# Scores of a two-component attention: two passes over stacked high and low parts per component, or three passes per component on half of the array's rows

## The chip, the cores and the metric

The kernel runs on one core of a Trainium2 chip. The metric is device time in microseconds for one execution of the whole step. The core has a matrix engine (PE; its weight loads are shown apart, as PEld), a vector engine (DVE), an activation engine (ACT), a general engine (POOL) and a queue for transfers (SP). Each engine takes its instructions in a fixed order, and engines wait for one another through semaphores.

## The reference

One layer of a streaming encoder is computed for 16 meta tokens, 2048 new frames and, apart, 32 frames of a running stream. The change touches the attention of the 2048 frames, above all the first line below:

```python
s = jnp.einsum('bqhcd,bkhcd->bchqk', q, k, preferred_element_type=f32) * SCALE
bias = rel_bias[rel_bucket(k_pos[None, :] - q_pos[:, None])]
s = s + bias; s = where(chunk_id(k_pos) <= chunk_id(q_pos), s, NEG)
p = jax.nn.softmax(s, axis=-1)
a = p[:, 0] - lam * p[:, 1]
return jnp.einsum('bhqk,bkhd->bqhd', a.astype(v.dtype), v)
```

There are 4 heads. A head's query and key have 128 numbers, which are two components c of 64 numbers each. Each component gives its own scores and softmax, and the second softmax, times lambda, is taken from the first. Around this stand an RMS norm, one input projection to 4096 columns, a gated short convolution, an output projection, a residual and a final norm. All is float32.

## The kernel before, in words

**Numbers in two parts.** A float32 operand of a product is split into a high part (a cast to the matmul type float32r) and a low part (what the cast left out). A product of a and b is then the sum of high·high, high·low and low·high. In the projections each of these is one matmul (line 212), three per 128 rows of contraction.

**Stages.** The 2048 frames are worked in four stages p of 512 frames, and in each stage the four heads h follow one another. `unit_a(h, p)` projects keys, values, queries and gates of one head for 512 frames. `attend(h, p, st)` then takes the four query tiles t of 128 frames, in two steps of two tiles. `unit_c` does the convolution of a column tile behind it.

**Scores.** For a query tile the visible key columns (16 meta and t + 1 tiles of 128) are cut into chunks of 144 to 512 columns; over the run there are 176 chunks. For each chunk and each component c `softmax_diff` calls `mm` (lines 427 to 429), which writes 128 queries x w keys to a PSUM bank of the pool `ps_s` (3 banks). DVE takes the row minimum (line 378, or 375 with the bias), ACT the exponential (line 379), which frees the bank. Later POOL and DVE (lines 382 and 383) join the two components, PE transposes the result (line 444), ACT and DVE split it (447 and 448), and lines 451 to 453 multiply it with the values.

**How a component's 64 rows fill 128.** The key tile `ks[c]` holds in its rows 0 to 63 the high part of component c and in its rows 64 to 127 the low part. The query tiles `q{c}0` and `q{c}1` hold the high part of component c in both halves, and the low part in both halves. So line 428 gives high·high + high·low in one pass over all 128 rows, and line 429 gives low·high + low·low: two full passes for each component and four for each chunk, 704 matmuls in all. To bring the parts into these rows, the loop behind `proj(CQ + h, ...)` issues 8 transfers `q<-r` of 64 rows per unit, and the loop behind `proj(CK + h, ...)` copies 64 rows at a time into `ks`, from the new keys (`ks<-r`) and, for p > 0, from the older ones in DRAM (`ks<-ksd`).

**What sets the order.** The program text gives dependencies. A list scheduler, which simulates the engines while it builds the program, chooses the order in which each engine's instructions stand. It works on single instructions: it may put other work between two matmuls which the text has next to each other. On the chip the order of each engine is fixed. All transfers are issued on SP by one helper, line 73.

Of the kernel before, what the change touches and what calls it, by code (L numbers as in the profile page):

```python
# [11 lines left out]
F32 = mybir.dt.float32  # L12
# [5 lines left out]
P = 128  # L18
# [29 lines left out]
def hybrid_step(ctx: ExitStack, tc: tile.TileContext, x, xT, ckT, cv, scT, rel_bias, norm_g, w_in,  # L48
# [9 lines left out]
    gp = pool("gp", 8)  # L58
    rp = pool("rp", 5)
    op = pool("op", 3)  # L60
# [16 lines left out]

# [1 line left out]
    ident = const.tile([P, P], F32, name="ident")  # L79
# [16 lines left out]

# [82 lines left out]

# [1 line left out]
    pre = {}  # L181
# [33 lines left out]

# [1 line left out]
    ksd = [dram.tile([2, P, NK], F32, name=f"ksd{h}", tag=f"ksd{h}") for h in range(H)]  # L217
# [6 lines left out]
    def unit_a(h, p):  # L224
# [13 lines left out]
        dma(kT_p[h, :, k0:k0 + kn], k32[:, :kn])  # L238
        ks = [kv.tile([P, NK], F32R, tag=f"ks{c}", name=f"ks{c}") for c in range(2)]
        for c in range(2):  # L240
            for i, src in enumerate((kh, kl)):
                if p > 0:
                    dma(ks[c][64 * i:64 * i + 64, :k0], ksd[h][i, 64 * c:64 * c + 64, :k0])
                dma(ks[c][64 * i:64 * i + 64, k0:k0 + kn], src[64 * c:64 * c + 64, :kn])
        if p < NQ - 1:
# [58 lines left out]

        qh, ql, q32 = r_tile(tw), r_tile(tw), g_tile(tw)
        qs = None
# [11 lines left out]
        proj(CQ + h, p, ev_q)  # L318
        qd = []
        for c in range(2):  # L320
            pair = []
            for i, src in enumerate((qh, ql)):
                q2 = one.tile([P, QT], F32R, tag=f"q{c}{i}", name=f"q{c}{i}")
                for half in range(2):
                    dma(q2[64 * half:64 * half + 64], src[64 * c:64 * c + 64, f0:f0 + QT])
                pair.append(q2)
            qd.append(pair)
        st["q"] = qd
        st["qs"] = qs
# [9 lines left out]

# [22 lines left out]
    def softmax_diff(pn, chunks, mm, bz):  # L362
        """chunks: [(first column, width)]; mm(c, ps, col, w) writes negated scores, bz is the negated bias of the
        last 512 columns; returns the chunks of a."""
        nch = len(chunks)
# [3 lines left out]
        for j, (c0, w) in enumerate(chunks):  # L369
            pr.append([pp.tile([P, 512], F32, tag=f"p{c}", name=f"p{c}", bufs=NP[c])[:pn, :w] for c in range(2)])  # L370
            for c in range(2):
                s = ps_s.tile([P, 512], F32, tag="s", name="s")[:pn, :w]
                mm(c, s, c0, w)
                if j == nch - 1:
# [11 lines left out]
    def chunks_of(t):  # L386
        """The columns (16 meta, then t + 1 tiles of 128) in pieces of at most 512, cut between tiles."""
        n = t + 1
# [26 lines left out]
    def attend(h, p, st):  # L415
        (q0h, q0l), (q1h, q1l) = st["q"]
        qd = st["q"]
        ks, (vh, vl), (z32, l1) = st["ks"], st["v"], st["z"]
        f0 = NM if p == 0 else 0
        o32, sq = o_tile(), o_tile()  # L420
        for b in range(2):
            tl = [4 * p + 2 * b, 4 * p + 2 * b + 1]
            aa = []
            for t in tl:
                qs = slice(P * (t - 4 * p), P * (t - 4 * p + 1))

                def mm(c, ps, col, w):
                    T.matmul(ps, lhsT=qd[c][0][:, qs], rhs=ks[c][:, col:col + w], start=True, stop=False)  # L428
                    T.matmul(ps, lhsT=qd[c][1][:, qs], rhs=ks[c][:, col:col + w], start=False, stop=True)  # L429
                ch = chunks_of(t)  # L430
                aa.append((ch, softmax_diff(P, ch, mm, st["bz"])))
# [34 lines left out]
    def attend_sample(h, st):  # L466
        """Rows 0..31: component 0 of the queries; rows 32..63: component 1."""
        kts, cvt, q2, (z32, l1) = st["kts"], st["cvt"], st["qs"], st["z"]
# [38 lines left out]

# [1 line left out]
    def unit_c(u, p):  # L509
# [54 lines left out]

# [1 line left out]
    bvs, bzd = [], []  # L566
# [22 lines left out]
    def prep_small():  # L589
# [32 lines left out]

# [1 line left out]
    y0 = [dram.tile([P, 512], F32, name=f"y0_{t}", tag=f"y0_{t}") for t in range(17)]  # L624
    ssq0 = const.tile([P, 17], F32, name="ssq0")

    def w_half(n):
# [3 lines left out]
        else:  # L631
            ks = [kv.tile([P, NK], F32R, tag=f"ks{c}", name=f"wo{c}") for c in range(2)]
            his = [ks[k // 4][:, 512 * (k % 4):512 * (k % 4 + 1)] for k in range(KT)]
            los = [r_tile(512) for _ in range(4)]
            los += [one.tile([P, QT], F32R, tag=f"q{c}{i}", name=f"wq{c}{i}") for c in range(2) for i in range(2)]
        for k in range(KT):
# [24 lines left out]
    def half_product(y, c, w, rows, ssq):  # L661
        """y (the residual) += cat @ w for 512 columns, and the sum of its squares."""
        chh, cll = c
# [52 lines left out]

# [1 line left out]
    after = (((0,), (1,), (2, 3), ()), ((0,), (1,), (2,), (3,)))  # L718
# [74 lines left out]
```

## Time and profile before

| what | before |
|---|---|
| median of 3 timed runs | 1342.75 us (1339.35 to 1343.84) |
| profiled execution, span from the first to the last instruction | 1338.5 us |
| PE busy | 1285.5 us, 96% of the span |
| PEld busy | 1104.2 us, 82% |
| DVE, ACT, POOL busy | 999.3, 717.6, 682.8 us |
| score matmuls, lines 428 and 429 | 352 and 352 |
| transfers `q<-r` | 128, 128 KB each, 4.7 us to landing (median) |

The page gives the profiled execution's span and no second time for it; the 4.25 us between the span and the median of the timed runs are what lies around it, and the spread of the runs. In the profile L428 is a line of the kernel before. A row names the written tile, an arrow and the tiles read, then the stationary operand's rows*columns (128*64 is 128 rows and 64 columns) and the moving operand's rows x columns. The duration of a matmul holds its way through the array and overlaps with the next one. What one costs in a stream is the distance between two starts, which is called the pitch below.

### The profile page before, as it was taken

Reading aid. Unit: us, or ns where it says so; the run is one execution under the profiler, and the core shown is the slowest. Engines: PE = TensorE matmul, PEld = TensorE weight load, DVE = VectorE, ACT = ScalarE, POOL = GpSimd, SP = SyncE. Lnnn points to the kernel's source line nnn. Section 1 sums busy time; section 2 is a strip of 40 time slices with the busy share of each in tenths; the row PEclk is TensorE's granted clock in tenths of the full one; section 3 lists DMA queues with packets and bytes.
Section 4 is the critical chain, followed back from the end, with each engine's and each line's share of the span. In section 5 each row is a group of like instructions: output and inputs, shape, how many; then the busy total and the mean of one; then the engine's idle time right before and its main releaser. Section 6 shows DMA issues by size and latency. Waiting matters only on the chain.

```text
span 1338.5 us, 21190 instructions
## 1 busy us (share of the span) xinstructions
PE 1285.5 (96%) x7058; PEld 1104.2 (82%) x7058; DVE 999.3 (75%) x2086; ACT 717.6 (54%) x1814; POOL 682.8 (51%) x619
## 2 busy tenths in 40 slices
PE   8899999999999999999999999998999999999997
PEld 6899999977878878878878788887887877878875
DVE  8677676668887958788888898786785895777753
ACT  5554454555564547454645566465554665674432
POOL 4555556455555663565566535564574573452200
PEclk9999999999999999999999999999999999999999
DMA  8754543894445377545453463636247348445851
GB/s 276 229 155 125 164 117 104 245 274 138 139 147 158 103 209 232 141 151 150 150 135 126 120 208 93 167 124 143 94 110 203 117 160 215 165 150 185 273 196 52
DMA packets 118670, 215.59 MB, mean 161 GB/s; under 512 B 19840, under 2 KB 48032, under 8 KB 118560
## 3 DMA queue, kind: packets, MB, share of 16 engines
q1 hardware_dynamic: 118560, 214.23, 54.7%
q8 instruction: 56, 0.92, 0.3%
q14 instruction: 54, 0.44, 0.1%
HBM read 145.62 MB, written 43.26 MB: 141 GB/s over the span
## 4 chain that ended last, share of the span: by engine, by line
PE 59%; DVE 16%; DMA 10%; issue 4%; ACT 4%; POOL 3%; SPq 2%; DVEq 0%; POOLq 0%; ACTq 0%
PE pj L212 37%; PE po L676 6%; DVE p L383 3%; PE s L428 3%; DMA q<-r 3%; PE s L429 3%; PE pt L444 3%; SPq L73 2%; DVE nm L378 2%; PE po L452 2%; PE po L453 2%; PE po L451 2%; DMA ks<-ksd 1%; ACT p L379 1%; POOL wl L192 1%
## 5 line engine op out<-in xcount | busy, mean ns | idle before, releaser
L212 PE MATMUL pj<-xh,wh 128*128 128x512 f32 (+2 forms) x1280 | 457.0, 358 | 4.0 <-ACT wh L191 1.3
L192 POOL TENSOR_TENSOR wl<-wr,wh 128x512 fp32r<-128x512 f32 x240 | 328.7, 1375 | 250.2 <-ACT wh L191 234.7
L212 PE MATMUL pj<-xl,wh 128*128 128x512 f32 (+2 forms) x1280 | 455.1, 356 | 0.8 <-DVE xl L140 0.8
L212 PE MATMUL pj<-xh,wl 128*128 128x512 f32 (+2 forms) x1280 | 454.7, 356 | 0.0
L379 ACT ACTIVATE p<-s,nm 128x384 f32<-128x384 f32 (+5 forms) x352 | 208.8, 595 | 186.8 <-DVE nm L378 135.1
L212 PEld LDWEIGHTS pj<-xh,wh 128*128 128x128 f32 x1280 | 243.2, 190 | 34.2 <-ACT bvec L586 2.0
L212 PEld LDWEIGHTS pj<-xh,wl 128*128 128x128 f32 x1280 | 242.9, 190 | 31.2 <-issue 1.3
L212 PEld LDWEIGHTS pj<-xl,wh 128*128 128x128 f32 x1280 | 243.4, 190 | 30.1 <-DVE xl L140 1.4
L191 ACT CAST wh<-wr 128x512 fp32r<-128x512 f32 x256 | 157.0, 616 | 129.4 <-PE pj L212 78.6
L383 DVE SCALAR_TENSOR_TENSOR p<-p,cf,p 128x384 f32<-128x384 f32 (+5 forms) x176 | 174.5, 1019 | 28.1 <-POOL p L382 27.8
L428 PE MATMUL s<-ks,q 128*128 128x384 f32 (+5 forms) x352 | 129.5, 375 | 26.8 <-DMA q<-r 10.0
L382 POOL TENSOR_SCALAR p<-p,cf 128x384 f32<-128x384 f32 (+5 forms) x176 | 125.0, 726 | 49.2 <-DVE cf L359 35.1
L378 DVE TENSOR_REDUCE nm<-s 128x1 f32<-128x400 f32 (+3 forms) x224 | 122.5, 557 | 28.2 <-PE s L429 27.9
L429 PE MATMUL s<-ks,q 128*128 128x384 f32 (+5 forms) x352 | 124.0, 354 | 2.0 <-DMA q<-r 2.0
L448 DVE TENSOR_TENSOR al<-pt,ah 128x512 fp32r<-128x512 f32 x144 | 97.0, 682 | 37.0 <-ACT ah L447 36.9
L656 POOL TENSOR_TENSOR cll<-ct,chh 128x512 fp32r<-128x512 f32 x40 | 53.9, 1353 | 113.6 <-ACT chh L654 105.4
L428 PEld LDWEIGHTS s<-ks,q 128*128 128x128 f32 x352 | 66.2, 190 | 42.5 <-issue 14.4
L447 ACT CAST ah<-pt 128x512 fp32r<-128x512 f32 x144 | 79.1, 585 | 40.8 <-PE pt L444 40.7
L375 DVE CUSTOM_DVE_ANT_0 s<-s,bz 128x512 f32<-128x512 f32 (+5 forms) x128 | 74.4, 585 | 17.9 <-PE s L429 13.5
L444 PE MATMUL pt<-ident,p 128*128 128x128 f32 x544 | 86.5, 274 | 0.0
L452 PE MATMUL po<-al,vh 128*128 128x256 f32 x288 | 84.2, 292 | 1.9 <-DVE al L448 1.7
L451 PE MATMUL po<-ah,vh 128*128 128x256 f32 x288 | 81.6, 283 | 0.0
(243 smaller groups left out, 2138.4 us busy)
## 6 DMA issues: line engine op xcount, KB each, us to landing
wr<-in_w_in SPq DMA_DIRECT2D x128, 512.0 KB, 4.1
q<-r SPq DMA_DIRECT2D x128, 128.0 KB, 4.7
ct<-cat SPq DMA_DIRECT2D x28, 512.0 KB, 4.8
out<-y SPq DMA_DIRECT2D x32, 256.0 KB, 3.4
ks<-ksd SPq DMA_DIRECT2D x16, 388.0 KB, 7.8
xr<-in_x SPq DMA_DIRECT2D x24, 256.0 KB, 4.8
out<-g SPq DMA_DIRECT2D x24, 256.0 KB, 4.5
xt<-in_xT SPq DMA_DIRECT2D x24, 256.0 KB, 4.2
```

Source lines behind the costliest of these rows:

```text
L191: S.copy(wh, wi)
L192: (V if (col in (CK, CV) if p == 0 else col in (CQ, CZ)) else G).tensor_tensor(wl, wi, f32(wh), op=ALU.subtract)
L212: T.matmul(ps, lhsT=a[:, k % 4], rhs=b[k][:, b0:b1], start=(k == 0 and i == 0), stop=(k == KT - 1 and i == 2))
L378: V.tensor_reduce(nm[:, c, j:j + 1], s, op=ALU.min, axis=AX.X)
L379: S.activation(pr[j][c], s, AF.Exp, bias=nm[:, c, j:j + 1], scale=-1.0, accum_out=l[:, c, j:j + 1])
L382: G.tensor_scalar(a0, a0, cf[:, 0, j:j + 1], 1.0, op0=ALU.mult, op1=ALU.mult)
L383: V.scalar_tensor_tensor(a0, a1, cf[:, 1, j:j + 1], a0, op0=ALU.mult, op1=ALU.add)
L428: T.matmul(ps, lhsT=qd[c][0][:, qs], rhs=ks[c][:, col:col + w], start=True, stop=False)
L429: T.matmul(ps, lhsT=qd[c][1][:, qs], rhs=ks[c][:, col:col + w], start=False, stop=True)
L444: T.transpose(pt[:, i, P * qi:P * (qi + 1)], cols(aa[qi], NM + P * (2 * j + i), P), ident)
L451: T.matmul(po, lhsT=vh[:, kt], rhs=ah[:, i], start=(kt == 0), stop=False)
L452: T.matmul(po, lhsT=vh[:, kt], rhs=al[:, i], start=False, stop=False)
```

## The change

The keys are no longer restacked: `ks[0]` is the high part and `ks[1]` the low part of all 128 rows, with component 0 in rows 0 to 63 and component 1 in rows 64 to 127, as the projection leaves them. The query parts are used as they are too, from a ring of their own (two tiles of each part), and the 8 copies `q<-r` per unit are gone. `mm` is called once for a chunk and writes the two banks of both components: three rounds (high·high, high·low, low·high; low·low is left out), and in each round one matmul on rows 0 to 63 for component 0 and one on rows 64 to 127 for component 1. The pool `rp`, in which the query parts were, goes from 5 to 4 buffers. Comments were taken out, so line numbers shift: the score matmuls are line 422 now, transposes 437, value products 444 to 446.

```diff
-    rp = pool("rp", 5)
+    rp = pool("rp", 4)
...
-        ks = [kv.tile([P, NK], F32R, tag=f"ks{c}", name=f"ks{c}") for c in range(2)]
-        for c in range(2):
-            for i, src in enumerate((kh, kl)):
-                if p > 0:
-                    dma(ks[c][64 * i:64 * i + 64, :k0], ksd[h][i, 64 * c:64 * c + 64, :k0])
-                dma(ks[c][64 * i:64 * i + 64, k0:k0 + kn], src[64 * c:64 * c + 64, :kn])
+        ks = [kv.tile([P, NK], F32R, tag=f"ks{i}", name=f"ks{i}") for i in range(2)]
+        for i, src in enumerate((kh, kl)):
+            if p > 0:
+                dma(ks[i][:, :k0], ksd[h][i, :, :k0])
+            dma(ks[i][:, k0:k0 + kn], src[:, :kn])
...
-        qh, ql, q32 = r_tile(tw), r_tile(tw), g_tile(tw)
+        qh, ql = (one.tile([P, NX + QT], F32R, tag=f"q{i}", name=f"q{i}", bufs=2)[:, :tw] for i in range(2))
+        q32 = g_tile(tw)
...
-        qd = []
-        for c in range(2):
-            pair = []
-            for i, src in enumerate((qh, ql)):
-                q2 = one.tile([P, QT], F32R, tag=f"q{c}{i}", name=f"q{c}{i}")
-                for half in range(2):
-                    dma(q2[64 * half:64 * half + 64], src[64 * c:64 * c + 64, f0:f0 + QT])
-                pair.append(q2)
-            qd.append(pair)
-        st["q"] = qd
+        st["q"] = qh, ql
...
-            for c in range(2):
-                s = ps_s.tile([P, 512], F32, tag="s", name="s")[:pn, :w]
-                mm(c, s, c0, w)
+            ss = [ps_s.tile([P, 512], F32, tag="s", name="s")[:pn, :w] for _ in range(2)]
+            mm(ss, c0, w)
+            for c, s in enumerate(ss):
...
-                def mm(c, ps, col, w):
-                    T.matmul(ps, lhsT=qd[c][0][:, qs], rhs=ks[c][:, col:col + w], start=True, stop=False)
-                    T.matmul(ps, lhsT=qd[c][1][:, qs], rhs=ks[c][:, col:col + w], start=False, stop=True)
+                def mm(ps, col, w):
+                    for i, (a, b) in enumerate(((qh, ks[0]), (qh, ks[1]), (ql, ks[0]))):
+                        for c in range(2):
+                            r = slice(64 * c, 64 * c + 64)
+                            T.matmul(ps[c], lhsT=a[r, qs], rhs=b[r, col:col + w], start=(i == 0), stop=(i == 2))
```

**The order on PE, third stage, before.** Rows of PE in the third stage (p = 2) before the change, where two components of one chunk stand; `ks_6768` and `ks_6769` are the stacked keys of component 0 and 1, `pj` is a projection:

```order
L212 MATMUL pj<-xh_6397,wh 128x512
L428 MATMUL s<-ks_6768,q_6874 128x512
L429 MATMUL s<-ks_6768,q_6877 128x512
L212 MATMUL pj<-xl_6398,wh 128x512
L212 MATMUL pj<-xh_6397,wl 128x512
L212 MATMUL pj<-xh_6403,wh 128x512
L428 MATMUL s<-ks_6769,q_6880 128x512
L429 MATMUL s<-ks_6769,q_6883 128x512
L212 MATMUL pj<-xl_6404,wh 128x512
```

The scheduler keeps a component's two passes together and puts projections between the two components.

**The same stage after the change.** `ks_6760` and `ks_6761` are now the high and the low part of the keys, `q_6821` and `q_6822` those of the queries. The two matmuls of one round read alike in these rows, so a round whose two halves follow each other is one row with x2, and a row without x2 is one half alone:

```order
L437 MATMUL pt<-ident,p_6603 128x128 x2
L422 MATMUL s<-ks_6760,q_6821 128x400 x2
L422 MATMUL s<-ks_6761,q_6821 128x400 x2
L422 MATMUL s<-ks_6760,q_6822 128x400 x2
L422 MATMUL s<-ks_6760,q_6821 128x384
L422 MATMUL s<-ks_6761,q_6821 128x384
L422 MATMUL s<-ks_6760,q_6822 128x384
L212 MATMUL pj<-xh_6377,wh 128x512
```

A little later in the same stage:

```order
L422 MATMUL s<-ks_6760,q_6821 128x512
L422 MATMUL s<-ks_6761,q_6821 128x512
L422 MATMUL s<-ks_6760,q_6822 128x512
L212 MATMUL pj<-xl_6336,wh 128x512
L212 MATMUL pj<-xh_6335,wl 128x512
L212 MATMUL pj<-xh_6341,wh 128x512
L212 MATMUL pj<-xl_6342,wh 128x512
L422 MATMUL s<-ks_6760,q_6821 128x512
L422 MATMUL s<-ks_6761,q_6821 128x512
L422 MATMUL s<-ks_6760,q_6822 128x512
L212 MATMUL pj<-xh_6341,wl 128x512
```

In the first piece one chunk stands as three rounds of two, and of the next chunk one component's three passes follow alone. In the second piece the two components of a chunk stand apart, with projections between them. In the whole order of PE 1056 score matmuls stand where 704 stood; 756 of them are rows without x2. They form 229 unbroken stretches; 105 of these are just three passes of one component. Counted along the stretches, 207 disjoint couples of neighbours lie on different halves of the rows, of 528 that the text writes.

**The order on SP, fourth stage.** Rows of SP before, where the keys of head 0 and its queries are copied:

```order
L73 DMA ks_10076<-ksd_131 64x1552
L73 DMA ks_10076<-r 64x512
L73 DMA q_10177<-r 64x512
L73 DMA q_10180<-r 64x512 x2
L73 DMA q_10183<-r 64x512 x2
L73 DMA q_10186<-r 64x512 x2
L73 DMA bz<-bz_300 128x512
```

and after:

```order
L73 DMA ks_10108<-ksd_131 128x1552
L73 DMA ks_10107<-ksd_131 128x1552
L73 DMA ks_10107<-r 128x512
L73 DMA ks_10108<-r 128x512
L73 DMA bz<-bz_300 128x512
```

The copies of queries are gone, and the keys come in transfers of 128 rows, half as many.

More of the change, by code (lines that the diff above doesn't have):

```diff
@@ L415, in attend @@
     def attend(h, p, st):
-        (q0h, q0l), (q1h, q1l) = st["q"]
-        qd = st["q"]
+        qh, ql = st["q"]
         ks, (vh, vl), (z32, l1) = st["ks"], st["v"], st["z"]
@@ L424, in attend @@
             for t in tl:
-                qs = slice(P * (t - 4 * p), P * (t - 4 * p + 1))
-                def mm(c, ps, col, w):
-                    T.matmul(ps, lhsT=qd[c][0][:, qs], rhs=ks[c][:, col:col + w], start=True, stop=False)
-                    T.matmul(ps, lhsT=qd[c][1][:, qs], rhs=ks[c][:, col:col + w], start=False, stop=True)
+                qs = slice(f0 + P * (t - 4 * p), f0 + P * (t - 4 * p + 1))
+                def mm(ps, col, w):
[3 more added lines that the diff above has]
+                            T.matmul(ps[c], lhsT=a[r, qs], rhs=b[r, col:col + w], start=(i == 0), stop=(i == 2))
                 ch = chunks_of(t)
@@ L634, in w_half @@
             los = [r_tile(512) for _ in range(4)]
-            los += [one.tile([P, QT], F32R, tag=f"q{c}{i}", name=f"wq{c}{i}") for c in range(2) for i in range(2)]
+            los += [one.tile([P, NX + QT], F32R, tag=f"q{i}", name=f"wq{i}", bufs=2)[:, :QT] for _ in range(2) for i in range(2)]
         for k in range(KT):
```

## The prediction

> **What bounds the kernel now.** I read the engines' shares on the page first, then its chain of waits, then what PE itself waited for, and last PE's timeline at the places where something like the new matmuls already runs.
>
> ```profile
> span 1338.5 us, 21190 instructions
> PE 1285.5 (96%) x7058; PEld 1104.2 (82%) x7058; DVE 999.3 (75%) x2086; ACT 717.6 (54%) x1814; POOL 682.8 (51%) x619
> ...
> PE 59%; DVE 16%; DMA 10%; issue 4%; ACT 4%; POOL 3%; SPq 2%; DVEq 0%; POOLq 0%; ACTq 0%
> PE pj L212 37%; PE po L676 6%; DVE p L383 3%; PE s L428 3%; DMA q<-r 3%; PE s L429 3%; PE pt L444 3%; SPq L73 2%; DVE nm L378 2%; PE po L452 2%; PE po L453 2%; PE po L451 2%; DMA ks<-ksd 1%; ACT p L379 1%; POOL wl L192 1%
> ```
>
> PE stands still for only 1338.5 - 1285.5 = 53 us, and no other engine is above 75%. So PE's own time sets the span, and a microsecond more on PE is nearly a microsecond more in all. The table of PE's waits says what can be had back:
>
> ```profile
> PE s L428 <- DMA q<-r: 10.0, 6, 3.2
> PE s L428 <- ACT p L379: 8.6, 11, 2.1
> PE s L428 <- DMA bz<-bz: 4.9, 1, 4.9
> ...
> PE s L429 <- DMA q<-r: 2.0, 5, 0.6
> ```
>
> The copies that the change drops hold PE up for 10.0 + 2.0 = 12 us.
>
> **What the score matmuls cost now.** The groups of line 428 by shape (line 429 has the same counts; 16 smaller ones are left out):
>
> ```profile
> L428 PE MATMUL s<-ks,q 128*128 128x384 f32 x128 | 47.2, 369 | 5.4 <-ACT p L379 5.3
> L428 PE MATMUL s<-ks,q 128*128 128x512 f32 x88 | 36.6, 416 | 1.5 <-ACT p L379 1.5
> L428 PE MATMUL s<-ks,q 128*128 128x400 f32 x88 | 33.2, 377 | 18.1 <-DMA q<-r 8.3 <-DMA bz<-bz 4.9 <-DMA ks<-r 2.5
> L428 PE MATMUL s<-ks,q 128*128 128x272 f32 x32 | 10.2, 318 | 1.7 <-DMA q<-r 1.7
> ```
>
> Their mean durations (369 ns) overlap with the next matmul, so the price is the pitch. PE's timeline (start, duration):
>
> ```profile
> 313.90 0.29 PE L428 MATMUL s<-ks,q 128*128 128x272 f32 x1
> 314.02 0.29 PE L429 MATMUL s<-ks,q 128*128 128x272 f32 x1
> 314.15 0.40 PE L212 MATMUL pj<-xh,wh 128*128 128x512 f32 x1
> 314.39 0.39 PE L212 MATMUL pj<-xl,wh 128*128 128x512 f32 x1
> 314.61 0.34 PE L428 MATMUL s<-ks,q 128*128 128x384 f32 x1
> 314.79 0.33 PE L429 MATMUL s<-ks,q 128*128 128x384 f32 x1
> 314.96 0.34 PE L428 MATMUL s<-ks,q 128*128 128x384 f32 x1
> ...
> 319.65 0.34 PE L428 MATMUL s<-ks,q 128*128 128x400 f32 x1
> 319.84 0.34 PE L429 MATMUL s<-ks,q 128*128 128x400 f32 x1
> 320.02 0.39 PE L212 MATMUL pj<-xh,wh 128*128 128x512 f32 x1
> ```
>
> From start to start 272 columns take 0.125 us, 384 take 0.175, 400 take 0.183, 512 take 0.23. With some 0.09 for the 16 small ones, line 428 costs 128 x 0.175 + 88 x 0.23 + 88 x 0.183 + 32 x 0.125 + 16 x 0.09 = 64.2 us, and with line 429 it is 128.4 us: 704 passes of 0.182 us on average.
>
> **Part 1: more passes.** The text writes three rounds where four passes stood, and a round is two matmuls. A pass is paid by its columns: if each half pass costs what a full pass of that width does, six stand where four stood. That is +64.2 us, before any overlap.
>
> **Part 2: how much of it overlaps.** The gain hangs on the two halves of a round running at once, and only neighbours on PE can do that. The order does not keep the rounds together: in 756 of 1056 rows one half stands without its partner, typically three passes of one component and then projections. 207 couples of neighbours lie on different halves. If each couple hides one pass whole, that gives back 207 x 0.182 = 37.7 us. A couple needs two weight loads, though. The price of a load shows where a matmul is too short to cover it:
>
> ```profile
> 106.55 0.29 PE L212 MATMUL pj<-xh,wh 128*128 128x272 f32 x1
> 106.67 0.18 PE L405 MATMUL pss<-sqh,ones_r 128*128 128x32 f32 x1
> 106.70 0.37 PE L212 MATMUL pj<-xl,wh 128*128 128x272 f32 x1
> 106.91 0.18 PE L406 MATMUL pss<-sql,ones_r 128*128 128x32 f32 x1
> ```
>
> The 32 columns of L405 with the 272 that follow take 106.91 - 106.67 = 0.24 us, and 272 alone take 0.125, so the short one costs 0.11: its load. Two loads in turn are 0.22, more than the 0.182 of the pass which they should hide behind. I take 0.04 x 207 = 8 us off the gain. It stands at -30 us; the ends are 0 (halves never overlap) and -37.7 (loads of two halves run at once).
>
> **Part 3: going into the half-row mode and out again.** There are 229 stretches of score matmuls between full ones. The trace has no float32r matmul on 64 rows, but it has plain float32 ones on half of the rows, next to full ones: the sample's transposes (64 rows) and its last value product (48 rows).
>
> ```profile
> 316.47 0.39 PE L212 MATMUL pj<-xl,wh 128*128 128x512 f32 x1
> 316.69 0.40 PE L212 MATMUL pj<-xh,wl 128*128 128x512 f32 x1
> 317.02 0.51 PE L494 MATMUL pts<-ident,as 64*128 64x64 f32 x5
> 317.47 0.50 PE L212 MATMUL pj<-xh,wh 128*128 128x512 f32 x1
> 317.80 0.40 PE L212 MATMUL pj<-xl,wh 128*128 128x512 f32 x1
> ...
> 322.36 1.00 PE L500 MATMUL pos<-o,cvt 128*128 128x64 f32 x8
> 323.29 0.43 PE L500 MATMUL pos<-o,cvn 48*128 48x64 f32 x2
> 323.65 0.50 PE L212 MATMUL pj<-xl,wh 128*128 128x512 f32 x1
> 323.99 0.39 PE L212 MATMUL pj<-xh,wl 128*128 128x512 f32 x1
> ```
>
> On the way in, the full matmul of 316.69 takes 0.33 us to the next start, not 0.23: +0.10. Inside, the two 48-row matmuls take 323.65 - 323.29 = 0.36; eight full ones of the same columns took 0.93, so two are worth 0.23: +0.13. On the way out, the first full matmul takes 0.33 and 0.34 to the next start: +0.11. A visit costs 0.34 us. A look at columns in place of rows shows that it is not any change of shape:
>
> ```profile
> 1300.91 0.39 PE L676 MATMUL po<-wq,cs 128*128 128x512 f32 x1
> 1301.14 0.40 PE L668 MATMUL po<-woh,chh 128*64 128x512 f32 x1
> 1301.37 0.40 PE L668 MATMUL po<-wol,chh 128*64 128x512 f32 x1
> ```
>
> Here the stationary operand goes from 128 to 64 columns and the pitch stays at 0.23. So a visit lies between 0 (if float32r on 64 rows behaves like this) and 0.34. I take 0.34, since both row cases agree and they share the thing that changes, the rows: 229 x 0.34 = +78 us.
>
> [...]
>
> **Part 4: what falls away.** The 12 us of waits for `q<-r` go: the queries now come from ACT and POOL alone, whose work the next projection on PE covers. Without that cover it would be the same 12 us again. The waits of L428 for the exponential (8.6 us) shrink, since a slower PE leaves ACT time; a chunk now wants two of the three banks at once, which works the other way. Between -8.6 and +8.6 I take -8.6, as the engines other than PE have no more work. The key copies on SP are half as many and hold nothing new up.
>
> **Sum.** 64.2 - 30 + 78 = +112 us on PE; less 12 and 8.6 it is +92 us. The profiled execution goes from 1338.5 to about 1431, and with the 4.25 us by which the timed median (1342.75) lies above the span, 1435 us.
>
> **Rivals.** (a) *The mode costs nothing* for float32r, as with columns in L668; against it stand L494 and L500. Then +64.2 - 30 - 20.6 = +14, which gives 1357. (b) *The halves do not overlap at all*, since no row of the trace shows two matmuls of full pitch at once: +64.2 + 78 - 20.6 = +122, 1465. (c) *Loads on the same half are not covered.* In the half-row mode each pass that is neither the first of a visit (229) nor the second of a couple (207) would pay 0.11 more: 620 x 0.11 = 68, 1503. Against it: the five transposes of L494 with their way out take only 0.45 us, 0.09 each, less than load and pass in turn. [...] (d) *Faster: the copies were worth more than PE's waits show.* The chain gives `q<-r` 3%, 40 us; with these gone in place of 12, and free visits, it is 14 - 28 = -14 us, 1329. It decides only if a visit costs below 14 / 229 = 0.06 us. For it speaks the chain, against it that PE visibly waited 12 us. (e) *The rounds run as written*, 528 couples at 0.22 with free visits: 116 in place of 128.4 us, less 20.6, 1310. The order has 207 couples, so this can hardly be.
>
> **How the numbers follow.** Forecast 0.70, (a) 0.12, (b) 0.09, (c) 0.04, (d) 0.04, (e) 0.01. The forecast's own range is 1390 to 1470: a visit of 0.2 us would bring 32 us less. To hold 8 in 10 the range reaches through (b) and takes in (a): 1357 to 1482. A difference of 0.3% is about what this measurement can tell from none. Faster are (d) and (e), 0.05. Within 0.3% falls only the lower edge of (a), 0.02. Slower: 0.93.
>
> **What would show it.** Score matmuls: 1056, on 64 rows, with a busy sum well above that of lines 428 and 429 now. In the timeline a full matmul ahead of a stretch shows a next start 0.10 us late, and the first projection after it 0.33 us to its next start, not 0.23. Three passes of one half follow each other at 0.175 us (384 columns); two halves start within a few hundredths of a microsecond of each other. PE's waits for `q<-r` are gone, and PE's share stays at 95% or more. Wrong I would be if first projections after a stretch kept 0.23 us (a), if couples stood a full pitch apart (b), if repeated halves stood 0.28 us apart (c), or if PE's idle time fell by 40 us (d).

## The result, and the profile after

The changed kernel takes 1422.34 us (median of 4 timed runs, 1420.95 to 1425.06). The kernel before, beside it, took 1342.62 us (1339.35 to 1343.84). The ratio is 1.0596, with a 95% interval of 1.0576 to 1.0615: 6% slower, and 13 us below the forecast of 1435. Two executions of kernels further below were granted a much lower clock than the others (0.74 and 0.88) and are left out of the medians and ratios.

The page of the changed kernel: span, engines' shares, granted clock, and the chain of waits by engine and by line.

```profile
span 1422.9 us, 21578 instructions
PE 1381.4 (97%) x7410; PEld 1105.4 (78%) x7410; DVE 1015.3 (71%) x2086; ACT 725.9 (51%) x1814; POOL 679.7 (48%) x619
...
PEclk9999999999999999999999999999999999999999
...
PE 81%; DVE 9%; DMA 4%; ACT 3%; issue 2%; POOL 1%; SPq 0%; DVEq 0%; ACTq 0%; POOLq 0%
PE pj L212 45%; PE s L422 12%; PE po L669 10%; PE pt L437 4%; PE po L445 2%; PE po L444 2%; PE po L446 2%; DVE p L374 1%; DMA wr<-in_w_in 1%; DMA ct<-cat 1%; PE ptv L271 1%; DVE xl L140 1%; ACT xh L139 1%; PE po L661 1%; DMA out<-y 0%
```

PE is busy for 95.9 us more than before, with 352 more matmuls, and stands still for 41.5 us instead of 53. Its share of the chain goes from 59% to 81%, and `q<-r` is gone from it. The other engines work nearly as long as before (DVE 16 us more, ACT 8 us). So the time went to PE, and the clock is not the reason: no slice is below nine tenths, and the mean granted clock is 0.992 (0.990 before).

What PE waited for in the changed kernel (in total, times, longest):

```profile
PE po L669 <- DVE y L670: 6.5, 4, 2.7
...
PE s L422 <- ACT p L370: 2.8, 4, 1.2
```

The waits of the scores for `q<-r` and for the exponential, 20.6 us before, have shrunk to 2.8 us. The two largest groups of the score matmuls, by shape (busy sum, mean ns):

```profile
L422 PE MATMUL s<-ks,q 64*128 64x384 f32 x384 | 76.8, 363 | 2.8 <-ACT p L370 2.8
L422 PE MATMUL s<-ks,q 64*128 64x512 f32 x264 | 74.9, 425 | 0.0
```

There are three times as many as in line 428, on 64 rows. The busy sum counts time that two matmuls share only once, so it does not tell a price. The price stands in PE's timeline, at a place where three passes of one component stand alone between projections:

```profile
762.73 0.39 PE L212 MATMUL pj<-xl,wh 128*128 128x512 f32 x1
762.96 0.40 PE L212 MATMUL pj<-xh,wl 128*128 128x512 f32 x1
763.28 0.96 PE L422 MATMUL s<-ks,q 64*128 64x512 f32 x3
764.18 0.50 PE L212 MATMUL pj<-xh,wh 128*128 128x512 f32 x1
764.51 0.39 PE L212 MATMUL pj<-xl,wh 128*128 128x512 f32 x1
```

From one projection to the next start it is 762.96 - 762.73 = 0.23 us. From the last full matmul to the first on half of the rows it is 0.32: +0.09. The three half passes take 764.18 - 763.28 = 0.90, where three pitches of 0.23 would be 0.69: +0.21. The first projection after them takes 0.33: +0.10. This visit costs 0.40 us beside its passes.

### The profile page after: what moved, and what is told of

The parts are those of the page before. It is cut to its first block, busy times and chain, and to the rows that moved or that the text cites. A ratio compares the mean times of both kernels' runs of the same rounds, so it can differ in the third digit from the quotient of the medians.

```text
span 1422.9 us, 21578 instructions
## 1 busy us (share of the span) xinstructions
PE 1381.4 (97%) x7410; PEld 1105.4 (78%) x7410; DVE 1015.3 (71%) x2086; ACT 725.9 (51%) x1814; POOL 679.7 (48%) x619
## 4 chain that ended last, share of the span: by engine, by line
PE 81%; DVE 9%; DMA 4%; ACT 3%; issue 2%; POOL 1%; SPq 0%; DVEq 0%; ACTq 0%; POOLq 0%
PE pj L212 45%; PE s L422 12%; PE po L669 10%; PE pt L437 4%; PE po L445 2%; PE po L444 2%; PE po L446 2%; DVE p L374 1%; DMA wr<-in_w_in 1%; DMA ct<-cat 1%; PE ptv L271 1%; DVE xl L140 1%; ACT xh L139 1%; PE po L661 1%; DMA out<-y 0%
## 5 line engine op out<-in xcount | busy, mean ns | idle before, releaser
L212 PE MATMUL pj<-xh,wh 128*128 128x512 f32 (+2 forms) x1280 | 462.1, 362 | 7.4 <-DVE g L325 3.2
L212 PE MATMUL pj<-xl,wh 128*128 128x512 f32 (+2 forms) x1280 | 462.5, 362 | 0.6 <-DVE xl L140 0.6
L422 PE MATMUL s<-ks,q 64*128 64x512 f32 (+5 forms) x1056 | 210.0, 375 | 2.8 <-ACT p L370 2.8
L374 DVE SCALAR_TENSOR_TENSOR p<-p,cf,p 128x384 f32<-128x384 f32 (+5 forms) x176 | 164.1, 957 | 21.1 <-POOL p L373 20.2
L422 PEld LDWEIGHTS s<-ks,q 64*128 64x128 f32 x1056 | 127.5, 184 | 66.2 <-issue 33.1
L373 POOL TENSOR_SCALAR p<-p,cf 128x384 f32<-128x384 f32 (+5 forms) x176 | 121.5, 706 | 84.6 <-DVE cf L350 56.8
L441 DVE TENSOR_TENSOR al<-pt,ah 128x512 fp32r<-128x512 f32 x144 | 97.0, 684 | 70.2 <-ACT ah L440 69.7
L369 DVE TENSOR_REDUCE nm<-s 128x1 f32<-128x384 f32 (+3 forms) x224 | 121.3, 559 | 11.5 <-PE s L422 11.1
L446 PE MATMUL po<-ah,vl 128*128 128x256 f32 x288 | 81.2, 282 | 0.0
```

Of the source, the lines that this page charges most:

```text
L212: T.matmul(ps, lhsT=a[:, k % 4], rhs=b[k][:, b0:b1], start=(k == 0 and i == 0), stop=(k == KT - 1 and i == 2))
L369: V.tensor_reduce(nm[:, c, j:j + 1], s, op=ALU.min, axis=AX.X)
L373: G.tensor_scalar(a0, a0, cf[:, 0, j:j + 1], 1.0, op0=ALU.mult, op1=ALU.mult)
L374: V.scalar_tensor_tensor(a0, a1, cf[:, 1, j:j + 1], a0, op0=ALU.mult, op1=ALU.add)
L422: T.matmul(ps[c], lhsT=a[r, qs], rhs=b[r, col:col + w], start=(i == 0), stop=(i == 2))
```

## The experiments

**The theory** was the sum of the prediction: more passes cost 64 us, visits to the half-row mode some 80, and neighbours on two halves give 30 to 40 back. **The rivals** still open after the result were that the slowdown comes from something else that the change brings (the order that the scheduler makes, the longer hold of two PSUM banks), that the halves do not truly overlap, and that the copies of queries were worth something which hid in the total.

### The parts in one and the same order of all engines

Two kernels issue every instruction of every engine in exactly the order of the changed kernel. Only the rows of the score matmuls differ, so that their scores are not those of the task: all 128 rows, so that there is no mode and no overlap, or rows 0 to 63 for both components, so that there are visits but no overlap.

```diff
                         for c in range(2):
-                            r = slice(64 * c, 64 * c + 64)
-                            T.matmul(ps[c], lhsT=a[r, qs], rhs=b[r, col:col + w], start=(i == 0), stop=(i == 2))
+                            T.matmul(ps[c], lhsT=a[:, qs], rhs=b[:, col:col + w], start=(i == 0), stop=(i == 2))
```

> The changed kernel with its 1056 score matmuls on all 128 rows (both components get the sum of the two, so the scores are wrong); every engine's instructions stand in exactly the same order as in the changed kernel. No visit to the half-row mode, no overlap. My theory (229 visits at 0.40 us, some 215 couples that hide 0.175 us each): 92 - 38 = 54 us less work on PE, of which the waits of the other engines may give some back: 1368 to 1385. Rival 'the loss is the number of passes alone, visits and couples cancel or cost nothing': 1422, no change against the changed kernel.

```diff
                         for c in range(2):
-                            r = slice(64 * c, 64 * c + 64)
+                            r = slice(0, 64)
```

> The same order again, with both components on rows 0 to 63 (component 1 gets the scores of component 0, so the result is wrong): the visits stay, and no neighbours lie on different halves. My theory: the changed kernel plus the overlap, 218 couples, 38 us: 1455 to 1460. Against the run on full rows it is the price of the visits alone: 92 us on PE, at least 70 in the span. Rival 'no real overlap': 1422.

Measured: 1389.95 us on full rows (ratio 1.0339, 1.0313 to 1.0364), 1460.17 us on one half (1.0873, 1.0847 to 1.0899). Their pages, full rows first:

```profile
span 1382.4 us, 21578 instructions
...
PE 1337.8 (97%) x7410; PEld 1158.8 (84%) x7410; DVE 1017.0 (74%) x2086; ACT 721.8 (52%) x1814; POOL 683.2 (49%) x619
```

```profile
span 1457.5 us, 21578 instructions
...
PE 1421.7 (98%) x7410; PEld 1146.0 (79%) x7410; DVE 1012.1 (69%) x2086; ACT 729.9 (50%) x1814; POOL 678.3 (47%) x619
```

The same place in PE's timeline in the three kernels: two small transposes, nine score passes (three of which can be second halves of couples), two projections. The row x9 merges six passes of 400 columns and three of 384. The changed kernel:

```profile
738.55 0.38 PE L449 MATMUL pm<-ident,p 128*16 128x128 f32 x2
738.86 1.34 PE L422 MATMUL s<-ks,q 64*128 64x400 f32 x9
740.13 0.50 PE L212 MATMUL pj<-xh,wl 128*128 128x512 f32 x1
740.46 0.39 PE L212 MATMUL pj<-xh,wh 128*128 128x512 f32 x1
```

Full rows:

```profile
721.85 0.38 PE L448 MATMUL pm<-ident,p 128*16 128x128 f32 x2
721.98 1.87 PE L421 MATMUL s<-ks,q 128*128 128x400 f32 x9
723.69 0.40 PE L212 MATMUL pj<-xh,wl 128*128 128x512 f32 x1
723.93 0.39 PE L212 MATMUL pj<-xh,wh 128*128 128x512 f32 x1
```

One half for both components:

```profile
756.75 0.38 PE L449 MATMUL pm<-ident,p 128*16 128x128 f32 x2
757.06 1.89 PE L422 MATMUL s<-ks,q 64*128 64x400 f32 x9
758.88 0.50 PE L212 MATMUL pj<-xh,wl 128*128 128x512 f32 x1
759.21 0.40 PE L212 MATMUL pj<-xh,wh 128*128 128x512 f32 x1
```

From the transposes' start to the second projection: 2.08 us on full rows, 2.46 on one half, 1.91 on two halves. One half against full rows is +0.38, a visit. Two halves against one half is -0.55, three couples of 0.18: each hides one pass of 400 columns (0.183) whole.

The same steps over the whole run, by the medians:

| step | us |
|---|---|
| before (in the same runs), 704 full passes | 1343.5 |
| 1056 full passes, copies gone | +46.5 |
| on 64 rows: 229 visits | +70.2 |
| on two halves, the changed kernel (1422.3) | -37.8 |

The steps are differences, so they add up by construction. The second and third change nothing but rows, so the visits and the overlap are measured alone. The first also has another order and no copies. The changed kernel was timed in other runs than its two relatives, beside a kernel before that took 0.8 us less; by the ratios its step is 37 us, give or take 4. 70.2 us over 229 visits is 0.31, less than the 0.40 that PE loses at each; the section on the rest of the time below says where the difference goes.

37.8 us over 207 couples would be 0.183 us each, just the mean pass. That agreement is an accident, since the two matmuls need not be neighbours. In the order of PE there are 23 stretches in which three passes of one half stand first and three of the other half behind them, which is one couple of neighbours. One of them in the changed kernel, with the projection behind it:

```profile
1036.90 0.97 PE L422 MATMUL s<-ks,q 64*128 64x512 f32 x6
1037.80 0.51 PE L212 MATMUL pj<-xl,wh 128*128 128x512 f32 x1
```

The same six passes with both components on one half:

```profile
1062.30 1.65 PE L422 MATMUL s<-ks,q 64*128 64x512 f32 x6
1063.88 0.50 PE L212 MATMUL pj<-xl,wh 128*128 128x512 f32 x1
```

Six passes take 0.90 us on two halves, as long as the three passes of one component above (763.28 to 764.18), and 1.58 on one half. The gain of 0.68 is three passes of 0.23, not the one of the couple: in the trace the fourth matmul of the order starts 0.01 us behind the first. Of the 98 stretches with both halves, 88 last as long as the passes of their longer half and 0.18 to 0.24 us more; the other ten last longer. Counted by the longer half, PE hides 46 us of passes, where the 207 couples would hide 36 by their own widths. (In the trace 218 pairs start within 0.03 us of each other, the count that stands in the expectation for one half.) So what overlaps cannot be read from neighbours. The 46 us on PE came out as 37.8 in the time.

### A visit alone, put into the kernel before

At the head of `mm`, once per chunk, one matmul of 16 columns on 64 rows goes ahead of the full passes, into columns that they overwrite; the control is the same matmul on 128 rows.

```diff
                 def mm(c, ps, col, w):
+                    if c == 0:
+                        T.matmul(ps[:, :16], lhsT=qd[0][0][:64, qs], rhs=ks[0][:64, col:col + 16], start=True, stop=True)
                     T.matmul(ps, lhsT=qd[c][0][:, qs], rhs=ks[c][:, col:col + w], start=True, stop=False)
```

> The kernel before, with one extra matmul of 64 rows and 16 columns ahead of each of the 176 chunks, into a bank which the next pass overwrites: 176 visits to the half-row mode and nothing else. My theory: 176 x 0.41 = +72 us, about 1415. 'Visits are free': the extra matmul costs its weight load alone, 176 x 0.11 = +19 us, 1362.

> The same extra matmul on all 128 rows: no visit, 176 weight loads more. Both theories: +19 us, about 1362. Its distance to the run with 64 rows is the price of 176 visits: 53 us by my theory, 0 by the rival.

Measured: 1403.29 us (ratio 1.0442, 1.0421 to 1.0463) and 1379.47 (1.0253, 1.0226 to 1.0279), against 1344.4 for the kernel before in the same runs: +59 and +35. PE's timeline at one of the 176 places, on 64 rows:

```profile
837.27 0.39 PE L212 MATMUL pj<-xh,wl 128*128 128x512 f32 x1
837.59 0.27 PE L429 MATMUL s<-ks,q 64*128 64x16 f32 x1
837.80 0.50 PE L430 MATMUL s<-ks,q 128*128 128x512 f32 x1
838.14 0.40 PE L431 MATMUL s<-ks,q 128*128 128x512 f32 x1
```

and on 128 rows:

```profile
817.53 0.39 PE L212 MATMUL pj<-xh,wl 128*128 128x512 f32 x1
817.77 0.17 PE L429 MATMUL s<-ks,q 128*128 128x16 f32 x1
817.79 0.48 PE L430 MATMUL s<-ks,q 128*128 128x512 f32 x1
818.11 0.39 PE L431 MATMUL s<-ks,q 128*128 128x512 f32 x1
```

From the start of the last projection to L431, both with two pitches of 0.23 in it, it is 0.87 against 0.58 us: 0.41 and 0.12 for the insertion. So the mode is paid where nothing overlaps and almost no columns run. In the whole, 176 x 0.29 = 51 us of difference came out as 24 us. The orders of these two kernels differ, so that this pair is no clean control of the whole time; the pair in one order above is.

### The couples put together, and put apart

The six matmuls of a chunk are chained, with priority in the scheduler: rounds as the text writes them, or all of one component and then all of the other.

```diff
-                    for i, (a, b) in enumerate(((qh, ks[0]), (qh, ks[1]), (ql, ks[0]))):
-                        for c in range(2):
+                    parts = ((qh, ks[0]), (qh, ks[1]), (ql, ks[0]))
+                    last = None
+                    with tc.high_priority():
+                        for i, c in ((0, 1), (0, 0), (1, 1), (1, 0), (2, 1), (2, 0)):
+                            a, b = parts[i]
...
+                            with (tc.issue_after(last.ins) if last is not None else ExitStack()):
+                                last = T.matmul(ps[c], lhsT=a[r, qs], rhs=b[r, col:col + w], start=(i == 0), stop=(i == 2))
```

For the couples apart the tuple is `((0, 1), (1, 1), (2, 1), (0, 0), (1, 0), (2, 0))`.

> The changed kernel, with the six score matmuls of a chunk chained in the order of the rounds and placed ahead of other work: 479 couples of neighbours on different halves instead of 207, and 208 visits to the half-row mode instead of 229. My theory (a couple hides one pass of 0.182 us whole, a visit costs 0.40 us, as the trace after the change shows): 272 x 0.182 + 21 x 0.40 = 58 us less than the changed kernel's 1422, about 1364, still slower than before. Rival 'halves do not really overlap, the two starts are only records': only the visits change, 1414. Rival 'visits are free, the loss is in slower halves': 50 us less, 1373.

> The changed kernel with the opposite chain: the three passes of one component, then the three of the other, so that only 61 couples are neighbours, in 302 visits. My theory: 146 couples fewer x 0.182 = +27 us and 73 visits more x 0.40 = +29 us, 1478 us. 'Visits are free': +27, 1449. 'No overlap': +29, 1451. Together with the run before this tells the two prices apart: two runs, two unknowns.

Measured: together 1434.13 us (ratio 1.0662, 1.0639 to 1.0686), apart 1469.63 (1.0927, 1.0906 to 1.0949). Apart came within 9 us of what was expected. It has 61 couples and 302 visits in place of 207 and 229; by the longer half it hides 19 us in place of 46, so 27 + 73 x 0.40 = 56 us more, and it is 47 us slower than the changed kernel. Together missed by 70 us: with 479 couples and 208 visits it hides 86 us by the longer half and should be 40 + 21 x 0.40 = 48 us faster than the changed kernel, but is 12 us slower. Its rows come from a second profile of the same kernel.

> The kernel of e1_couples_together once more, since its profile was taken at a clock of 0.74 and shows nothing of its timed runs (1430 to 1436 us at their fastest), which missed the theory's 1364 by some 70 us. If the theory of couples and visits holds on PE, this profile shows couples a few hundredths of a microsecond apart and visits of 0.40 us, and the 70 us stand elsewhere: as waits of PE or as pitches made longer by something that I have not named. If couples cost more when there are many, the pitch inside the stretches shows it (more than 0.175 us for a couple of 384 columns).

Measured: 1433.04 us (1.0666, 1.0638 to 1.0693). Its page and the largest of PE's waits:

```profile
span 1430.9 us, 21614 instructions
...
PE 1360.8 (95%) x7410; PEld 1086.5 (76%) x7410; DVE 1000.7 (70%) x2086; ACT 718.9 (50%) x1814; POOL 677.6 (47%) x619
...
PEclk9999999999999999999999999999979989869999
```

```profile
PE s L426 <- ACT p L370: 19.2, 24, 3.3
```

PE is busy for 20.6 us less than in the changed kernel, though part of that busy time now runs at a clock of 0.50 (below), and it stands still for 70 us instead of 41.5. A chained chunk wants both of its banks at its start, of three in all, and the exponential must have emptied them: 19.2 us in 24 waits, against 2.8 us in 4. And the clock row is no longer flat. In stretches of 2 us (length, busy time and matmuls of PE, weight loads, DVE, ACT, POOL, then the granted clock):

```profile
1142.00:1144.00 2.00, 0.89 (x5) 0.53 (x6) 2.00 (x6) 1.91 (x7) 0.00 (x0) 1.00 0.30 117
1144.00:1146.00 2.00, 0.68 (x6) 0.32 (x2) 1.86 (x7) 1.38 (x5) 1.26 (x1) 0.87 0.01 6
1146.00:1148.00 2.00, 0.01 (x2) 0.01 (x2) 2.00 (x4) 1.44 (x4) 1.98 (x3) 0.50 0.54 143
1148.00:1150.00 2.00, 2.00 (x7) 1.25 (x8) 2.00 (x3) 0.60 (x2) 2.00 (x3) 0.50 0.39 119
```

PE is busy for only 0.89 + 0.68 = 1.57 of 4 us, the clock falls to 0.50, and when work is there again PE does 7 matmuls in 2 us of full work, where the 40 us from 1160 to 1200, at a clock of 1.00, have 215. If the clock is either 1.00 or 0.50, with means between only where it changes, as in the stretches read here, a mean of 0.967 over 1430.9 us means that 2 x 0.033 x 1430.9 = 94 us ran at half clock; in the changed kernel (0.992) it was 23 us. Both are estimates. So the gain of the couples was lost twice, to waits for banks and to a slower clock behind the waits. Whether the priority was the cause of it, by pushing the exponentials' work back, is tested by the same chain without it:

```diff
-                    with tc.high_priority():
+                    if True:
```

> As e1 (the rounds of a chunk chained), without placing them ahead of other work: 468 couples in 222 visits. PE's own work is 1.7 us above e1's (11 couples fewer at 0.182, 14 visits more at 0.40 would be 7.6). Theory on e1's miss (its couples wait for the second bank, and a PE that waits drops to half its clock): with other work let in ahead, PE waits less for the exponential than e1's 19 us, and the time is 1380 to 1420. Rival 'the couples themselves cost more': as e1, 1433.

Measured: 1459.09 us (1.0861, 1.0833 to 1.0888), with 468 couples and 222 visits. The largest of its waits on PE:

```profile
PE s L426 <- ACT p L370: 31.6, 28, 2.6
```

So the priority was not the cause: without it, PE waits longer for the same banks.

### Other banks for the couples

Since the chain needs two banks at a time, the pool of the scores was cut into two pairs of banks. The kernel's pools hold 2 + 3 + 2 + 1 = 8 banks, and the fourth one for the scores was taken from another pool: in the first kernel from the transposes, in the second from the projections, with two chunks chained behind each other.

```diff
-    ps_s = pool("ps_s", 3, space=bass.MemoryType.PSUM)
-    ps_t = pool("ps_t", 2, space=bass.MemoryType.PSUM)
+    ps_s = pool("ps_s", 2, space=bass.MemoryType.PSUM)
+    ps_t = pool("ps_t", 1, space=bass.MemoryType.PSUM)
...
-            ss = [ps_s.tile([P, 512], F32, tag="s", name="s")[:pn, :w] for _ in range(2)]
-            mm(ss, c0, w)
+            if j % 1 == 0:
+                todo = chunks[j:j + 1]
+                sp = [ps_s.tile([P, 2, 512], F32, tag="s", name="s") for _ in todo]
```

> The changed kernel with the two banks of a chunk allocated together (two pairs of banks; the transposes give up one of their two banks) and the rounds chained: 500 couples of 528, 152 visits. By the prices of the theory 293 x 0.182 + 77 x 0.40 = 84 us less than 1422: 1338, if the lost bank costs nothing. Rival 'something in couples costs more, as e1 hints': as e1, 1400 to 1435. Rival 'the transposes' one bank makes PE wait': the 144 pairs of transposes wait up to 1 us each for their split, 1400 or more, and the waits show it at the transposes.

> Two chunks chained into one visit where the banks allow it (two pairs of banks for scores; the projections give up one of their two banks): 514 couples, 134 visits, the least work on PE of all versions with half rows: 64.2 - 514 x 0.182 + 134 x 0.40 = +24 us against the kernel before. If the lost bank cost nothing this would be about 1345, level with the kernel before. Theory: every projection now waits for its only bank to be emptied (0.5 to 1 us, 176 projections), so 1400 to 1480.

Measured: 1480.28 us (1.1024, 1.0985 to 1.1064) and 1584.0 us (1.1798, 1.1757 to 1.1839). The couples were there, 500 and 514 of 528, and the visits fell to 152 and 134. The waits on PE of the first:

```profile
PE po L454 <- ACT ah L450: 26.2, 22, 4.5
PE s L431 <- ACT p L376: 17.3, 16, 4.4
PE po L455 <- DVE al L451: 13.5, 18, 3.9
```

and of the second:

```profile
PE po L679 <- DVE y L680: 22.9, 19, 3.1
PE pj L212 <- DVE g L552: 20.8, 12, 3.7
```

With one bank for the transposes PE waits for their split (lines 450 and 451 there), with one for the projections it waits for their readers. Each bank taken away costs more than the couples bring. Whether they would pay with more banks was not tried.

### The copies of queries by themselves

The kernel before without the copies: the scores are taken from the query parts as they lie. And the kernel before with the same tiles, written by ACT, POOL and DVE in place of the transfers. Both have an order of their own.

```diff
-                for half in range(2):
-                    dma(q2[64 * half:64 * half + 64], src[64 * c:64 * c + 64, f0:f0 + QT])
...
+        st["q"] = [(qh[:, f0:f0 + QT], ql[:, f0:f0 + QT])] * 2
```

> The kernel before, with the 128 copies of queries left out: both components read the query parts as the projection leaves them, on all 128 rows, so the scores are wrong and the work of PE is the same. It prices the copies alone. My theory (PE waited 12 us for them, and 20 us more of waits at L428 are near them): 12 to 20 us faster, 1323 to 1331. Rival (d) of the prediction, the copies were worth the chain's 3%: 40 us, 1303. Rival 'hidden anyway, the next wait takes their place': 1343, no change.

```diff
+                for half in (c, 1 - c):
+                    src, dst = slice(64 * c, 64 * c + 64), slice(64 * half, 64 * half + 64)
+                    S.copy(qd[c][0][dst, s0 - f0:s1 - f0], q32[src, s0:s1])
+                    (G if half != c else V).tensor_tensor(qd[c][1][dst, s0 - f0:s1 - f0], q32[src, s0:s1], f32(qd[c][0][src, s0 - f0:s1 - f0]), op=ALU.subtract)
```

> The kernel before, with the query tiles of both components written by ACT, POOL and DVE straight from the projection's result, half of the rows at a time, in place of a cast, a subtraction and eight transfers. Per unit ACT has three casts of half tiles more (0.6 us each), POOL and DVE have two subtractions each in place of POOL's one. All of it lies beside PE, which is the bound. Theory: the waits for the copies go as in the run without them, less what the engines' longer way costs (about 2 us per unit, under the next projection): 1325 to 1335, faster than before. Rival: ACT's extra 1.8 us per unit delays the exponentials, so PE waits for banks: 1345 to 1360.

Measured: 1347.93 us without the copies (1.0036, 1.0015 to 1.0056) and 1375.13 with the copies on engines (1.0225, 1.0191 to 1.0259). The largest wait of PE without the copies:

```profile
PE s L420 <- DMA ks<-ksd: 8.1, 4, 3.2
```

and with the copies on engines:

```profile
PE s L424 <- DMA ks<-ksd: 13.4, 5, 4.4
PE s L424 <- ACT p L375: 9.1, 14, 2.1
PE pj L212 <- DVE g L330: 7.0, 3, 3.4
```

The 12 us of waits for `q<-r` brought nothing when the copies went. The scores wait for the copies of keys then, which before held PE up for 2.5 us only. On ACT, POOL and DVE the copies cost 32 us: PE waits for the copies of keys, for the exponential and for readers of projections.

### Where the rest of the time goes

To compare kernels of different orders, PE's work was counted from each trace: every matmul at its pitch by columns (512 columns 0.231 us, 400 0.183, 384 0.175, 272 0.125; square transposes 0.109), less, in each stretch, the passes of the half that has less to do, plus 0.40 us for each visit. The count is good to a few microseconds. The rest, up to the time from the first to the last matmul (the span less some 12 us), is waits and slow clock.

| kernel | work counted, us | rest, us |
|---|---|---|
| before | 1244 | 83 |
| changed | 1353 | 58 |
| full rows, same order | 1308 | 62 |
| one half, same order | 1400 | 45 |
| visit put into the kernel before | 1334 | 55 |
| its control | 1263 | 97 |
| halves apart | 1410 | 48 |
| without the copies | 1244 | 90 |
| couples together (second profile) | 1305 | 114 |
| couples together, no priority | 1312 | 131 |
| pairs of banks, transposes with one | 1273 | 189 |
| pairs of banks, projections with one | 1265 | 301 |

In the three kernels of identical order the rest shrinks as PE's own work grows: 62, 58 and 45 us at 1308, 1353 and 1400. From full rows to one half, 92 us more work (229 x 0.40) came with 17 us less rest, and the span grew by 75; from one half to two, 46 us less work came with 13 us more rest, and the span shrank by 35. That the other engines get time to deliver beside a slower PE is the likely reason, but it was not tested by itself. Between different orders it is no rule: the control of the visit has more work than the kernel before, and more rest.

## Why the prediction was right, and where it was off

The forecast, that the visits to the half-row mode and the added passes outweigh the overlap, holds: each of the three terms was found with its sign, the visits and the overlap by runs in one order, the added passes by their pitches.

**Part 1, more passes:** by the pitches of the trace 64.4 us, predicted 64.2. A half pass costs what a full one of its width does: nine passes on one half took 1.82 us, where six pitches of 0.183 and three of 0.175 are 1.62, and three took 0.90, where three pitches are 0.69. What is left over, 0.20 and 0.21, belongs to the visit and does not grow with the passes.

**Part 2, the overlap:** 30 us predicted; PE hides 46, and 37.8 of it show in the time. Two steps failed. The one is "only neighbours on PE can do that": six passes of 512 columns, three and three in the order, took 0.90 us, and a stretch lasts as long as its longer half. The other is "Two loads in turn are 0.22, more than the 0.182 of the pass which they should hide behind". Couples step at 0.165 to 0.18 us for 384 and 400 columns and hide the pass whole, so the loads of the two halves do not run in turn. That the upper end of the part's own range, 37.7, is so near to the 37.8 is luck: it counts neighbours and takes PE's gain for the gain in time.

**Part 3, the visits:** 0.40 us each on PE, 92 us in all, where 0.34 and 78 were taken; that a visit costs was right, and the size was off. The way in (+0.09 to +0.10) and the way out (+0.10) are as predicted from the rows of plain float32. The stay inside costs +0.21, not +0.13: the first half pass and the last each give up about 0.10. In the span it came to 70.2 us, since PE's waits shrank beside it.

**Part 4, the waits:** the rest fell by 25 us (83 to 58), where 20.6 were taken, but not for the reason given. The step that failed is "The 12 us of waits for `q<-r` go": the rows went, but without the copies alone the time did not fall (1347.93 us, the interval wholly above 1), and the rest was 90. What fits the rows is the step which the text used for the exponential only, "a slower PE leaves ACT time" (8.6 us there before, 2.8 now): without the copies and with 64 us more work on PE, in the kernel of full rows, the rest was 62. The orders differ, so this is not shown by itself.

**The sum:** passes 64.4, visits 92, overlap -46 and rest -25 give +85, and the span grew by 84.4; predicted were 92. On PE alone it is +110, where +112 was forecast: the visits were off by +14 and the overlap by -16, and that they cancelled is luck. The other 5 us of the miss are the 4.25 us between span and median: here the median lies 0.6 below the span. The profiled execution before was the fastest of its kernel and the one after the slowest, so the medians lie 79.7 us apart and not 84.4.

**Rivals.** (a) is refuted by the identical orders (70.2 us) and by the single visit (0.41 against 0.12 us), (b) by them too (37.8 us). (c) is refuted by the spacing of repeats on one half, 0.174 to 0.176 us for 384 columns and 0.23 for 512: full passes of these widths took 0.175 and 0.23 before, so the 0.11 more for a load is not paid. (d) is refuted: without the copies the time is 0.4% above that of the kernel before. (e) was given its couples, 479 of 528, and did not come out either; "with free visits" was one failed condition of it, and the other is that couples need two banks at the same time.

How the lost gain of the couples together divides can be estimated. Against the changed kernel the rest grew by 56 us. PE stands still for 29 us more (70 against 41.5). Of the time at half clock PE was busy for 69 us, against 20 in the changed kernel; in the changed kernel projections of 512 columns start 0.43 us apart at a clock of 0.50 (423.91 to 424.34) and 0.23 apart at 1.00, so 0.20 of every 0.43 of these 49 us is lost, about 23. Together that is 52 of the 56 us. It is an estimate: no run has the gaps without the slow clock behind them.

## What to carry to other kernels

Count the visits to the half-row mode as an item of its own: here a stretch of matmuls on 64 rows among full ones paid about 0.40 us, with 16 columns in it (0.41), three passes (0.40) or nine (0.38), and beside that 88 of 98 stretches with both halves lasted as long as their longer half. What it saves are the passes of the shorter half, so at 0.40 us against 0.183 for a pass of 400 columns each half needs more than two of them to break even, before the added passes. Read from the order, not from the text, what stands of each half in each stretch, next to each other or not, and check that the banks for both halves can be free at once. A wait on the bounding engine that goes away is a gain only if nothing stands behind it: taken out here, 12 us of waits were worth nothing.

## What the runs showed of the hardware that was not expected

Two matmuls on the two halves of the rows start 0.01 us apart (1036.90 us in the changed kernel; 218 pairs start within 0.03), and no time for a second weight load shows beside them: nine passes of 400 and 384 columns in one visit took 1.27 us with three couples, and 1.82 us on one half. They need not stand next to each other in the order: with three passes of one half ahead of three of the other, all six of 512 columns took 0.90 us, as long as three.

A visit costs four separate delays of 0.09 to 0.11 us. At the visit of 763.28 us in the changed kernel the last full matmul takes 0.32 us to the next start instead of 0.23, the first half-row matmul 0.34, the last 0.32 and the first full one after it 0.33; the second of the three half-row matmuls takes 0.23 (starts 763.28, 763.62, 763.85). The cost is there with 16 columns, too: 0.41 us, against 0.12 on 128 rows.

With the couples together the clock fell to 0.50 after a few microseconds in which PE mostly stood still, and stayed there although PE was busy again. PE was busy for 1.57 of the 4 us from 1142 to 1146, and the clock had a mean of 1.00 and then 0.87 there; it was 0.50 from 1146 to 1154, with PE busy for 5.55 of the last 6 us, and 1.00 again from 1160 to 1200. If it went from 1.00 to 0.50 at once, the mean of 0.87 puts the fall at about 1145.5 us, an estimate. At a clock of 0.50 projections of 512 columns stand 0.43 us apart in place of 0.23, as the changed kernel shows. So the gaps of the chained couples cost more than their own length.
